# Swapping the order of two preparations before each group's first added pair, and reloading a spilled tile two pairs later

## The chip, the cores and the metric

The kernel runs on one core of a Trainium2 chip. The metric is the device time of one execution in microseconds (us). Three executions of the kernel before took 1149.12, 1149.59 and 1150.76 us; their median, 1149.59 us, is the time before. A separate execution, the one that was profiled, took 1150.18 us; its trace spans 1148.2 us from the first to the last instruction, at a granted TensorE clock of 0.997.

## The reference

One layer of an encoder on 256 tokens of width 2048, all in float32:

```
h   = rmsnorm(x, norm1_gain);  proj = h @ w_in
x   = x + concat(attention(proj), hgrn2(proj)) @ w_out
h2  = rmsnorm(x, norm2_gain)
ff  = silu(h2 @ w_gate) * (h2 @ w_up)        # 2048 -> 5632, twice
x   = x + ff @ w_down                        # 5632 -> 2048
out = rmsnorm(x, final_gain)
```

The change touches only the last three products, `w_gate`, `w_up` and `w_down`, which fill the trace from about 449 us on.

## The kernel before

**Products in parts.** Every float32 operand is held as a rounded part and a rest: `wh` and `wl` for weights, and likewise for activations. A product is three matmuls: rounded with rounded, rounded with rest, rest with rounded. Forming `wh` is a copy on ACT (ScalarE, L88); forming `wl` is a subtraction on DVE (VectorE, L89) that reads the `wh` just formed. Both handle 128x1024 elements at a time, half of a pair. Four tiles of each kind rotate.

**Pairs and groups.** The weights come in pairs: 1 MB, two 128-row slices of two 512-column blocks. The two blocks of activations (tokens 0-127, 128-255) and the two column blocks give four PSUM sums c00, c01, c10, c11. A group is a pass over all pairs of two column blocks: eleven groups `gated` for gate and up (eight pairs each), then two groups `down` (22 pairs each). A pair has one of three kinds:

- "d", ordinary: load `raw`, form `wh` and `wl` for both halves, 24 matmuls.
- "s", a pair of seven products (in the manner of Strassen) with sums and differences `ta`, `tb` of the weights formed on DVE (L747 to L749), 21 matmuls into the c and m banks.
- "a", added: as "d", but DVE forms nothing. `begin` loads the pair into `rawa`, ACT writes its negated rounded copy into `low` (L716), and a DMA issued on POOL (GpSimd) adds the weights from HBM onto it (L717), which leaves the rest. `prepare_begun` later forms `wh` from `rawa` (L727). Its matmuls with `wh` come first (16), those with `low` last (8).

Groups 1 to 10 of `gated` run `full`, that is a4, s0, d5, s1, a6, s2, s3, d7 (kind, then pair number); group 0 has ordinary pairs only. At the end of a group come the last pair's 24 matmuls, block by block, and the read-out of the banks: `spread` (L841 on ACT, L842 to L845 on DVE) reads the m banks, `block` (L852, L858, L860) the c banks.

**What sets the order.** `run_groups` prepares one pair ahead: while the matmuls of item i are written, item i+1 is prepared by `prepare`. For an "a" item, `begin` is called one item earlier still, in the `prepare` of the item before it. Each engine executes its own instructions in one order that a scheduler derives from this program text; the two L716 copies are held to their place in the text. All large loads are issued by SP in one chain (`dma`), each when its buffer is free: `raw` has three buffers, `rawa` one. A load that waits for its buffer holds up those behind it. The DMAs into `low` are issued by POOL; `low` has three buffers.

**The spilled tile.** The sum after `w_out`, `x2` (2 MB), is written to HBM early in group 0 of `gated`, because its space is needed for `hs`, and read back by two 1 MB loads `x<-x2d` at the start of `down`. It is first used at L909, after the seven "s" pairs of the first `down` group.

Of the kernel before, what the change touches and what calls it, by code (L numbers as in the profile page):

```python
# [8 lines left out]
F32 = mybir.dt.float32  # L9
# [7 lines left out]
P = 128  # L17
S = 256
NT = S // P
D = 2048  # L20
# [25 lines left out]
def hybrid_block(ctx: ExitStack, tc: tile.TileContext, x, xT, w_in, w_out, w_gu, w_down,  # L46
# [8 lines left out]
    res = ctx.enter_context(tc.tile_pool(name="res", bufs=1))  # L55
# [25 lines left out]
    def dma(o, i):  # L81
        with ExitStack() as st:
            if prev:
                st.enter_context(tc.issue_after(prev[-1]))
            prev.append(nc.sync.dma_start(o, i).ins)
# [118 lines left out]
    for t in range(NT):  # L204
        a = abp.tile([P, 4, P], F32, name=f"aT{t}")
# [234 lines left out]
    for g in range(2):  # L440
        vxs.append(abp.tile([P, 2, W], F32R, tag="t4", name="vx", bufs=NT4))
        v1s.append(abp.tile([P, W], F32, tag="ht", name="v1", bufs=3))
        pool, tag = (pacc, "acc") if g == 0 else (paux, "aux")
# [150 lines left out]
    x2 = res.tile([P, NT, D], F32, tag="res", name="x2")  # L594
# [68 lines left out]
    def row_sums(dst, hi, lo):  # L663
        n = hi.shape[1] // 2
        a = dn.tile([P, 2, 2, S], F32, tag="ta", name="a")[:, 0:n]
        sm = dn.tile([P, 4, 2, P], F32, tag="tb", name="sm")[:, :, 0:n]
        nc.vector.tensor_tensor(a, hi.rearrange("p (j k) t -> p j k t", k=2).bitcast(F32),
                                lo.rearrange("p (j k) t -> p j k t", k=2).bitcast(F32), ALU.add)
        a11, a12, a21, a22 = a[:, :, 0, 0:P], a[:, :, 1, 0:P], a[:, :, 0, P:S], a[:, :, 1, P:S]
        nc.vector.tensor_tensor(sm[:, 0], a21, a22, ALU.add)  # L670
        nc.vector.tensor_tensor(sm[:, 1], sm[:, 0], a11, ALU.subtract)
        nc.vector.tensor_tensor(sm[:, 2], a11, a21, ALU.subtract)
        nc.vector.tensor_tensor(sm[:, 3], a12, sm[:, 1], ALU.subtract)
        split(dst[:, 0], dst[:, 1], sm)
# [98 lines left out]
    def run_groups(groups, following=None):  # L773
        todo = [(gr, n) for gr in groups for n in range(len(gr.items))]

        def prepare(i):
            if i + 1 < len(todo):
                gr, n = todo[i + 1]
                if gr.items[n][0] == "a":
                    gr.begin(gr.items[n][1])  # L780
            gr, n = todo[i]
            return gr.prepare(*gr.items[n])

        steps, held = groups[0].ready or prepare(0), []
        for i, (gr, n) in enumerate(todo):
            ahead = None
            if n + 1 == len(gr.items):
                if i + 1 < len(todo):
                    ahead = prepare(i + 1)
                elif following is not None:  # L790
                    following.ready = following.prepare(*following.items[0])
                gr.run_blocks(held + steps, gr.block)
                held = []
                gr.end()
            elif n + gr.hold >= len(gr.items):
                held = held + steps
            else:
                gr.run(steps)
                seen = sum(1 for kind, _ in gr.items[:n + 1] if kind == "s")
                if gr.items[n][0] == "s" and seen == gr.ns:  # L800
                    gr.spread()
            if i + 1 < len(todo):
                steps = ahead or prepare(i + 1)
            gr.between(n)
# [6 lines left out]
    x2d = spill.tile([NT, P, D], F32, name="x2d")  # L811
    own = {"low": gu}
# [13 lines left out]
    def ff_split(ff, j):  # L826
        for i in range(2):
            pt = pair_transpose(lambda t: ff[:, t, :], i * 256)
            hi, lo, k = f_home(4 * j + 2 * i)
            ks = slice(k, k + 2)  # L830
            split(hi[:, ks, :], lo[:, ks, :], pt.rearrange("p j t n -> p j (t n)"))

    class Gated(Group):
# [31 lines left out]
        def between(self, n):  # L865
            if n == 0:
                if self.g == 0:
                    second_end()
                    for t in range(NT):
                        dma(x2d[t], x2[:, t, :])  # L870
                    own["hs"] = res.tile([P, 2, 4, FASTU, P], F32R, tag="res", name="hs")
                else:
                    ff_split(gated[self.g - 1].ff, self.g - 1)
            if self.g == 0 and 1 <= n <= (FASTU + 1) // 2:
                j0, j1 = 2 * n - 2, min(2 * n, FASTU)
                row_sums(own["hs"][:, :, :, j0:j1, :], h2[:, 2 * j0:2 * j1, 0, :], h2[:, 2 * j0:2 * j1, 1, :])
# [13 lines left out]
    def load_fg():  # L890
        fg = own["fg"]
        dma(fg, fgain.to_broadcast([P, D]))
        nc.scalar.activation(warm, fg[:, 0:1], AF.Square)
        nc.scalar.activation(warm, warm, AF.Sqrt)

    class Down(Group):
# [44 lines left out]
        def between(self, n):  # L941
            if self.g == 0:
                if n == 0:
                    x2 = own["x2"] = res.tile([P, NT, D], F32, tag="res", name="x2")
                    for t in range(NT):
                        dma(x2[:, t, :], x2d[t])
                    gup.__exit__(None, None, None)
                    late = ctx.enter_context(tc.tile_pool(name="late", bufs=1))
                    own.update(f_last=late.tile([P, 2, 4, S], F32R, name="f_last"), fg=late.tile([P, D], F32, name="fg"))
                    ff_split(gated[-1].ff, len(gated) - 1)  # L950
                elif n <= FAST // 2:
                    ks = slice(4 * (n - 1), 4 * n)
                    row_sums(sf[:, n - 1], fh[:, ks, :], fl[:, ks, :])
                elif n == FAST // 2 + 1:
                    load_fg()

    def finish(ps, t):
        x2 = own["x2"]
# [94 lines left out]
```

## Time and profile before

| What | Value |
|---|---|
| Median of three runs (lowest, highest) | 1149.59 us (1149.12, 1150.76) |
| Profiled execution, its span | 1150.18 us, 1148.2 us |
| PE busy | 1131.7 us, 99% of the span, 5381 matmuls |
| DVE busy | 916.4 us, 80% |
| ACT busy | 699.6 us, 61% |
| Moved by DMA | 248.95 MB, 217 GB/s over the span |
| One `gated` group, 1 to 10 | 42.55 us; PE busy 42.22 us, DVE 38.5 us, DMA engines 80% of the time |

PE is TensorE's matmuls; PEld is its loading of weights. A matmul of 512 columns is listed with some 390 ns, but successive ones start 227 ns apart, because they overlap; so a stall is read from the distance of two starts, not from the busy share. "Idle before, releaser" in square brackets names what an engine waited for.

### The profile page before, as it was taken

To read this page: it belongs to the slowest core of one execution; us is meant where nothing else is said; L and a number is where in the kernel's file an instruction comes from. 1 tells how busy PE (TensorE), PEld (TensorE's weight loads), DVE (VectorE), ACT (ScalarE), POOL (GpSimd) and SP (SyncE) were. 2 spreads that over 40 slices of the span, in tenths; PEclk is the share of its full clock that TensorE was granted. 3 is DMA by queue.
4 is the path that set the end of the run, shared out by engine and by line. 5 is a ranking of instruction groups with operands and counts; after the bars stand their busy time and mean duration, and the time that the engine had idled before them with its cause. 6 is when DMAs were issued, how large, how long until landed. Compare 5 with 4: busy or idle time off the path is not lost.

```text
span 1148.2 us, 14288 instructions
## 1 busy us (share of the span) xinstructions
PE 1131.7 (99%) x5381; PEld 941.1 (82%) x5381; DVE 916.4 (80%) x1166; ACT 699.6 (61%) x900; POOL 53.7 (5%) x73
## 2 busy tenths in 40 slices
PE   9999999999999999999999999999999999999996
PEld 7888888888888888887888878878878877888885
DVE  7577768947746666589889889889989998898885
ACT  7565656847645555576676676676676565555553
POOL 3300000000000000000010010010010000000000
PEclk9999999999999999999999999999999999999998
DMA  9655445554744547878778778778788756555552
GB/s 316 248 199 181 176 147 184 183 184 147 287 153 160 191 163 277 271 219 218 261 255 225 259 254 236 259 245 244 256 241 241 265 206 220 211 191 211 199 214 74
DMA packets 41397, 248.95 MB, mean 217 GB/s; under 512 B 4848, under 2 KB 5360, under 8 KB 15344
## 3 DMA queue, kind: packets, MB, share of 16 engines
q1 hardware_dynamic: 35568, 227.06, 54.1%
q0 software_dynamic: 5760, 20.97, 10.5%
q8 instruction: 42, 0.69, 0.2%
q14 instruction: 27, 0.22, 0.1%
HBM read 243.82 MB, written 4.19 MB: 216 GB/s over the span
## 4 chain that ended last, share of the span: by engine, by line
PE 93%; DVE 3%; ACT 1%; DMA 1%; issue 1%; SPq 0%; ACTq 0%; DVEq 0%
PE c L704 43%; PE m L704 13%; PE acc L169 10%; PE acc L171 5%; PE acc L146 5%; PE acc L144 5%; PE acc L145 5%; DVE wl L89 2%; PE vps L145 1%; PE ptr L315 1%; PE vps L146 1%; PE vps L144 1%; DMA x2d<-x 1%; ACT wh L88 1%; DMA raw<-in_w_in_dram 0%
## 5 line engine op out<-in xcount | busy, mean ns | idle before, releaser
L89 DVE TENSOR_TENSOR wl<-raw,wh 128x1024 fp32r<-128x1024 f32 (+1 forms) x378 | 418.8, 1122 | 134.5 <-ACT wh L88 133.2
L88 ACT ACTIVATE wh<-raw 128x1024 fp32r<-128x1024 f32 (+1 forms) x378 | 362.4, 972 | 229.5 <-PE c L704 79.2
L704 PE MATMUL c<-wh,h 128*128 128x512 f32 x928 | 275.7, 390 | 0.0
L704 PEld LDWEIGHTS c<-wh,h 128*128 128x128 f32 x928 | 173.4, 188 | 37.5 <-ACT wh L88 1.7
L169 PE MATMUL acc<-hx,wh 128*128 128x512 f32 x512 | 179.7, 395 | 0.0
L171 PE MATMUL acc<-hx,wl 128*128 128x256 f32 x512 | 142.6, 278 | 0.0
L704 PE MATMUL c<-wl,h 128*128 128x512 f32 x304 | 119.6, 394 | 3.1 <-DVE wl L89 3.1
L169 PEld LDWEIGHTS acc<-hx,wh 128*128 128x128 f32 x512 | 96.0, 188 | 21.7
L88 ACT ACTIVATE wh<-ta 128x1024 fp32r<-128x1024 f32 x55 | 58.4, 1061 | 71.4 <-PE c L704 36.3
L88 ACT ACTIVATE wh<-tb 128x1024 fp32r<-128x1024 f32 x55 | 58.3, 1061 | 63.0 <-PE c L704 34.8
L171 PEld LDWEIGHTS acc<-hx,wl 128*128 128x128 f32 x512 | 96.4, 188 | 0.1
L704 PE MATMUL c<-wh,fh 128*128 128x512 f32 x230 | 89.6, 390 | 0.4 <-ACT wh L88 0.2
L704 PE MATMUL c<-wl,fh 128*128 128x512 f32 x230 | 89.5, 389 | 0.0
L704 PE MATMUL c<-wh,fl 128*128 128x512 f32 x230 | 89.5, 389 | 0.0
L704 PE MATMUL m<-wh,hs 128*128 128x512 f32 x240 | 82.0, 389 | 0.0
L89 DVE TENSOR_TENSOR wl<-ta,wh 128x1024 fp32r<-128x1024 f32 x55 | 67.2, 1223 | 18.1 <-ACT wh L88 18.0
L704 PEld LDWEIGHTS c<-wl,h 128*128 128x128 f32 x304 | 57.0, 188 | 19.5 <-DVE wl L89 7.5
L89 DVE TENSOR_TENSOR wl<-tb,wh 128x1024 fp32r<-128x1024 f32 x55 | 67.2, 1221 | 6.7 <-ACT wh L88 4.5
L747 DVE TENSOR_TENSOR ta<-raw 128x1024 f32<-128x1024 f32 x55 | 67.2, 1221 | 6.4 <-DMA raw<-in_w_down_dram 5.8
L717 POOL DMA_DIRECT2D low<-in_w_gu_dram x40 | 34.6, 873 | 731.1 <-ACT low L716 571.2
L704 PEld LDWEIGHTS m<-wh,hs 128*128 128x128 f32 x240 | 45.1, 188 | 9.6
L704 PEld LDWEIGHTS c<-wh,fh 128*128 128x128 f32 x230 | 43.1, 188 | 10.0 <-ACT wh L88 0.6
(289 smaller groups left out, 1845.6 us busy)
## 6 DMA issues: line engine op xcount, KB each, us to landing
raw<-in_w_gu_dram SPq DMA_DIRECT2D x68, 1024.0 KB, 7.2
raw<-in_w_in_dram SPq DMA_DIRECT2D x48, 1024.0 KB, 4.8
raw<-in_w_down_dram SPq DMA_DIRECT2D x44, 1024.0 KB, 4.8
rawa<-in_w_gu_dram SPq DMA_DIRECT2D x20, 1024.0 KB, 6.4
low<-in_w_gu_dram POOLq DMA_DIRECT2D x40, 512.0 KB, 7.5
raw<-in_w_out_dram SPq DMA_DIRECT2D x16, 1024.0 KB, 4.8
raw<-in_w_in_dram SPq DMA_DIRECT2D x12, 512.0 KB, 6.0
raw<-in_w_in_dram SPq DMA_DIRECT2D x8, 256.0 KB, 5.0
```

The source lines that it names most:

```text
L88: nc.scalar.activation(hi, src, AF.Copy)
L89: nc.vector.tensor_tensor(lo, src, hi.bitcast(F32), ALU.subtract)
L144: nc.tensor.matmul(ps[t], lhsT=xh[:, tok], rhs=wh, start=kt == 0, stop=False)
L145: nc.tensor.matmul(ps[t], lhsT=xh[:, tok], rhs=wl, start=False, stop=False)
L146: nc.tensor.matmul(ps[t], lhsT=xl[:, tok], rhs=wh, start=False, stop=kt == kts - 1)
L169: nc.tensor.matmul(ps[m].rearrange("p j t -> p (j t)"), lhsT=wh[:, col], rhs=both, start=kt == 0, stop=False)
L171: nc.tensor.matmul(ps[m][:, 0, :], lhsT=wl[:, col], rhs=rhs[:, kt, 0, :], start=False, stop=kt == KD - 1)
L315: nc.tensor.transpose(pt[:, j, t, :], nat(t)[:, n0 + j * P:n0 + (j + 1) * P], ident)
L704: nc.tensor.matmul(self.bank[n], lhsT=a, rhs=b, start=self.left[n] == self.total[n], stop=self.left[n] == 1)
L717: nc.gpsimd.dma_start(out=wl.rearrange("p b n -> p (b n)"), in_=self.src[self.base + j, :, 2 * k * W:2 * (k + 1) * W], accum_op=ALU.add)
L747: nc.vector.tensor_tensor(ta, raw[:, 1:3], raw[:, 0:2], ALU.subtract)
```

## The change

In `prepare`, an ordinary pair is now prepared (its load, its two `wh`, its two `wl`) before the `begin` of a following added pair; before, `begin` came first. For the other kinds the order is as it was, so a6, which follows s1, is begun as before. The place where "d" is followed by "a" is the end of a group: d7 of groups 0 to 9, followed by a4 of the next group. The reload of `x2` moves from after pair 0 to after pair 2 of the first `down` group.

```diff
         def prepare(i):
-            if i + 1 < len(todo):
-                gr, n = todo[i + 1]
-                if gr.items[n][0] == "a":
-                    gr.begin(gr.items[n][1])
             gr, n = todo[i]
-            return gr.prepare(*gr.items[n])
+            nxt, m = todo[i + 1] if i + 1 < len(todo) else (None, 0)
+            steps = gr.prepare(*gr.items[n]) if gr.items[n][0] == "d" else None
+            if nxt and nxt.items[m][0] == "a":
+                nxt.begin(nxt.items[m][1])
+            return steps or gr.prepare(*gr.items[n])
...
                 if n == 0:
-                    x2 = own["x2"] = res.tile([P, NT, D], F32, tag="res", name="x2")
-                    for t in range(NT):
-                        dma(x2[:, t, :], x2d[t])
                     gup.__exit__(None, None, None)
...
                 elif n == FAST // 2 + 1:
                     load_fg()
+                if n == 2:
+                    x2 = own["x2"] = res.tile([P, NT, D], F32, tag="res", name="x2")
+                    for t in range(NT):
+                        dma(x2[:, t, :], x2d[t])
```

The first place is ACT at the end of a group, from the last `tb` of s3 to the first `wh` of s0 in the next group. `wh<-raw ... x2` are the two halves of d7, `low<-rawa` and `wh<-rawa` belong to a4. Before:

```order
L88 ACTIVATE wh<-tb 128x1024
L841 COPY ff<-m_4956 128x512
L716 ACTIVATE low<-rawa 128x1024 x2
L88 ACTIVATE wh<-raw 128x1024 x2
L727 ACTIVATE wh<-rawa 128x1024 x2
L88 ACTIVATE wh<-raw 128x512
```

and after:

```order
L88 ACTIVATE wh<-tb 128x1024
L841 COPY ff<-m_4956 128x512
L88 ACTIVATE wh<-raw 128x1024 x2
L716 ACTIVATE low<-rawa 128x1024 x2
L727 ACTIVATE wh<-rawa 128x1024 x2
L858 ACTIVATE ff<-ff,rst_3175 128x512
```

The two negated copies go two places back, and the two `wh` of d7 two places forward.

The second place is DVE at the same point: `uv` and `ff` at L842 to L845 read the m banks of the group that ends, L852 its c banks. Before:

```order
L89 TENSOR_TENSOR wl<-tb,wh 128x1024
L842 TENSOR_TENSOR uv<-m_4958,ff 128x512
L89 TENSOR_TENSOR wl<-raw,wh 128x1024
L843 TENSOR_TENSOR uv<-m_4957,uv 128x512
L844 TENSOR_TENSOR ff<-m_4959,uv 128x512
L89 TENSOR_TENSOR wl<-raw,wh 128x1024
L845 TENSOR_TENSOR uv<-m_4957,ff 128x512
L852 TENSOR_TENSOR ff<-c_4891,ff 128x512
L852 TENSOR_TENSOR uv<-c_4892,uv 128x512
L852 TENSOR_TENSOR ff<-c_4893,ff 128x512
L860 SCALAR_TENSOR_TENSOR ff<-uv,rst_3175,ff 128x512
L852 TENSOR_TENSOR uv<-c_4894,uv 128x512
```

and after:

```order
L89 TENSOR_TENSOR wl<-tb,wh 128x1024
L89 TENSOR_TENSOR wl<-raw,wh 128x1024 x2
L842 TENSOR_TENSOR uv<-m_4958,ff 128x512
L843 TENSOR_TENSOR uv<-m_4957,uv 128x512
L844 TENSOR_TENSOR ff<-m_4959,uv 128x512
L852 TENSOR_TENSOR ff<-c_4891,ff 128x512
L845 TENSOR_TENSOR uv<-m_4957,ff 128x512
L852 TENSOR_TENSOR uv<-c_4892,uv 128x512
L852 TENSOR_TENSOR ff<-c_4893,ff 128x512
L860 SCALAR_TENSOR_TENSOR ff<-uv,rst_3175,ff 128x512
L89 TENSOR_TENSOR wl<-raw,wh 128x512
L852 TENSOR_TENSOR uv<-c_4894,uv 128x512
```

Both `wl` of d7 now stand ahead of L842; before, they stood behind it and between the others. The first `wl` of the next pair (128x512, s0) now stands ahead of the read of c_4894, which is c11.

The third place is SP's queue from the last groups of `gated` into `down`; `x` is the tile `x2`. Before:

```order
L85 DMA raw<-in_w_gu_dram 128x2048 x3
L85 DMA rawa<-in_w_gu_dram 128x2048
L85 DMA raw<-in_w_gu_dram 128x2048 x4
L85 DMA raw<-in_w_down_dram 128x2048 x2
L85 DMA x_7752<-x2d 128x2048 x2
L85 DMA raw<-in_w_down_dram 128x2048 x5
L85 DMA fg<-in_fgain_dram 128x2048
```

and after:

```order
L85 DMA raw<-in_w_gu_dram 128x2048 x2
L85 DMA rawa<-in_w_gu_dram 128x2048
L85 DMA raw<-in_w_gu_dram 128x2048 x4
L85 DMA raw<-in_w_down_dram 128x2048 x4
L85 DMA x_7858<-x2d 128x2048 x2
L85 DMA raw<-in_w_down_dram 128x2048 x3
L85 DMA fg<-in_fgain_dram 128x2048
```

Ahead of `rawa` for a4 there is now one load more, that of d7 (x4 instead of x3 between two `rawa`, and x2 instead of x3 after it); the reload has moved behind two more loads of `down`. PE's order changes with DVE's: d7's matmuls now run block by block, where before the scheduler had put four matmuls with `wh` ahead of the first with `wl`.

## The prediction

> **What bounds the kernel now.** I read the page first, for the engine that carries the span.
>
> ```profile
> span 1148.2 us, 14288 instructions
> PE 1131.7 (99%) x5381; PEld 941.1 (82%) x5381; DVE 916.4 (80%) x1166; ACT 699.6 (61%) x900; POOL 53.7 (5%) x73
> ...
> PE 93%; DVE 3%; ACT 1%; DMA 1%; issue 1%; SPq 0%; ACTq 0%; DVEq 0%
> ```
>
> PE carries 93% of the chain. A change elsewhere is worth only the PE stalls that it removes or makes, so I looked next for these, in the list of waits and, by place, in the chain in order of time.
>
> ```profile
> PEld c L704 <- DVE wl L89: 7.8, 11, 0.8
> ...
> DVE uv L842 <- PE m L704: 15.9, 9, 1.8
> ```
>
> ```profile
> 517.71 1.23 DVE wl L89
> ...
> 687.86 1.23 DVE wl L89
> ...
> 858.01 1.23 DVE wl L89
> ```
>
> The chain leaves PE for a `wl` once per group, nine times from 517.71 to 858.01, every 42.55 us: at the ends of groups 1 to 9. L842 waits for PE nine times as well. The timeline of one such place, with weight loads left out, shows why:
>
> ```profile
> 684.26 1.23 DVE L89 TENSOR_TENSOR wl<-tb,wh 128x1024 fp32r<-128x1024 f32 x1
> 684.60 2.01 ACT L716 ACTIVATE low<-rawa 128x1024 fp32r<-128x1024 f32 x2
> 686.06 1.80 POOL L717 DMA_DIRECT2D low<-in_w_gu_dram  x2 [21.35 <-ACT low L716]
> 686.50 2.00 ACT L88 ACTIVATE wh<-raw 128x1024 fp32r<-128x1024 f32 x2
> 687.25 0.69 DVE L842 TENSOR_TENSOR uv<-m,ff 128x512 f32<-128x512 f32 x1 [1.77 <-PE m L704]
> 687.45 1.35 PE L704 MATMUL c<-wh,h 128*128 128x512 f32 x5
> 687.86 1.22 DVE L89 TENSOR_TENSOR wl<-raw,wh 128x1024 fp32r<-128x1024 f32 x1
> 688.40 2.00 ACT L727 ACTIVATE wh<-rawa 128x1024 fp32r<-128x1024 f32 x2
> 689.13 0.51 PE L704 MATMUL c<-wl,h 128*128 128x512 f32 x1 [0.33 <-DVE wl L89]
> 689.47 0.63 PE L704 MATMUL c<-wh,h 128*128 128x512 f32 x2
> ...
> 697.42 1.98 PE L704 MATMUL c<-low,h 128*128 128x512 f32 x8
> ```
>
> ACT makes a4's two negated copies (684.60) before d7's `wh` (686.50). DVE, done with `tb` at 685.49, has nothing it may do: its next instruction, L842, needs the last m bank and starts at 687.25. d7's first `wl` follows at 687.86 and ends at 689.08, and PE, which has used up its four `wh` matmuls, starts at 689.13.
>
> The size of the stall: matmuls start (1.98 - 0.39) / 7 = 0.227 us apart in the last row. Of the five from 687.45 the last starts at 687.45 + (1.35 - 0.39) = 688.41, so the next was due at 688.64 and came at 689.13: 0.49 late. The one after it came 0.34 later instead of 0.227: 0.11 more. Together **0.61 us per group, 5.5 us in nine groups**. This is the most that the first edit can give.
>
> **The change part by part.**
>
> *d7 ahead of a4's copies.* Nothing is added or removed. ACT's two pairs of copies change places: both take 1.9 us from start to start (684.60 to 686.50 to 688.40), so d7's `wh` move to 684.60 and 685.55, L716 to 686.50 and 687.45, and L727 stays at 688.40. DVE can form d7's `wl` at 685.7 to 688.1, in the time in which it now waits for the m bank. PE wants the first at about 687.9 and the second at 688.6. So the stall goes: -5.5 us. Group 10, which no added pair follows, already runs in the new order and shows it:
>
> ```profile
> 898.38 2.36 DVE L89 TENSOR_TENSOR wl<-raw,wh 128x1024 fp32r<-128x1024 f32 x2 [0.21 <-ACT wh L88]
> ...
> 900.13 0.62 PE L704 MATMUL c<-wh,h 128*128 128x512 f32 x2
> ...
> 900.59 0.39 PE L704 MATMUL c<-wl,h 128*128 128x512 f32 x1
> 900.65 0.69 DVE L842 TENSOR_TENSOR uv<-m,ff 128x512 f32<-128x512 f32 x1
> ```
>
> Two `wl` stand before L842, and PE passes from 900.13 to 900.59 at its 0.23 us per matmul.
>
> *SP's order.* d7's load no longer stands behind `rawa`, which waits for L727 of a6 to free its buffer.
>
> ```profile
> 668.27 0.68 DVE L749 TENSOR_TENSOR tb<-raw,tb 128x512 f32<-128x512 f32 x1
> ...
> 672.05 0.33 SPq L85 DMA_DIRECT2D rawa<-in_w_gu_dram  x1
> 672.47 10.60 SPq L85 DMA_DIRECT2D raw<-in_w_gu_dram  x3
> ```
>
> Its own buffer, last read by s1, is free at 668.95; so it goes 3.5 us earlier, and `rawa` still goes at 672.05. ACT wants `rawa` at 686.50 now. This costs nothing by itself. In group 10, where no `rawa` stands in the way, a6's copies meet such an early load already, and no wait of PE for a copy stands in the list of waits.
>
> *The copies `low` come later.* This is the price. Both are issued by POOL after L716, so 1.90 us later, while PE comes to them 0.61 us sooner. PE wants the second at its fifth `low` matmul, 697.42 + 4 x 0.227 = 698.33. When it is issued, and what such copies take from issue to landing (least, median, most), stands in the tile's own view; here it is for this place (the second issue precisely 0.94 us after 686.06, at 687.00), for the ends of two earlier groups, and for a6's second copy alone:
>
> ```profile
> L717 POOL DMA_DIRECT2D low<-in_w_gu_dram x2: 847/854/860, 686.1 to 687.0; - x2
> ...
> DMA to landing us min/median/max: 5.3/7.1/8.8
> ```
>
> ```profile
> DMA to landing us min/median/max: 5.6/6.5/7.3
> ```
>
> ```profile
> DMA to landing us min/median/max: 5.8/7.4/9.0
> ```
>
> ```profile
> L717 POOL DMA_DIRECT2D low<-in_w_gu_dram x1: 870/870/870, 663.8 to 663.8; - x1
> ...
> DMA to landing us min/median/max: 10.5/10.5/10.5
> ```
>
> The second copy has 698.33 - 687.00 = 11.33 us now and 11.33 - 1.90 - 0.61 = **8.82 us after**. The first copy lands after 5.3 to 5.8 us and has more in hand. The second takes 7.3 to 9.0 us at a group's end, and 10.5 us in a6, where SP issues a load beside it:
>
> ```profile
> 663.77 0.33 SPq L85 DMA_DIRECT2D raw<-in_w_gu_dram  x1
> ...
> 690.42 0.33 SPq L85 DMA_DIRECT2D rawa<-in_w_gu_dram  x1
> ```
>
> At a group's end the next load is issued 690.42 - 687.00 = 3.4 us after the second copy, in a6 at the same time. After the change L727 still frees `rawa` at 690.4, so the distance is 690.4 - 688.9 = 1.5 us. Bounds: 7.3 us if the loads do not touch the copy; 9.4 us on a straight line between (0, 10.5) and (3.4, 8.05, the mean of 7.3 and 8.8). If each us of earlier load costs the copy one us, it is 10.5 - 1.5 = 9.0 us. I take 9.0, because it is also near this place's own 8.8. PE then waits 9.0 - 8.82 = 0.18 us in each of nine groups, **+1.6 us**; bounds 0 and 9 x (9.4 - 8.82) = +5.2 us. The Trainium skill ("DMA: Bandwidth & Descriptors", "Anatomy of one DMA") gives a fit for copies of this path, 2.0 us and the bytes at 436 GB/s: 3.2 us for 0.5 MB, and PE would wait for neither, a sum of -5.5 us. The trace does not agree; its shortest copy here took 5.3 us, and the measured ones decide.
>
> *The banks' read-out.* L842 starts at about 688.0 instead of 687.25, but the chain of DVE then has no `wl` in it. The narrowest point is c11, which the next group's PE needs.
>
> ```profile
> 691.96 0.63 ACT L88 ACTIVATE wh<-raw 128x512 fp32r<-128x512 f32 x1 [1.56 <-PE c L704]
> ```
>
> s0's first `wh` waits for d7's last use of a buffer, the 21st instead of the 15th matmul of d7, so it comes at some 692.6; its `wl` at 693.3 stands ahead of c11's read, which ends near 694.6. PE writes that bank 31 matmuls after d7's start at 687.67, at 694.7. A margin of 0.1 us: 0, at worst a few tenths, and not on top of the wait for `low`, which comes 2.9 us later on the same PE.
>
> *The reload.* Two loads move behind those of down's pairs 2 and 3.
>
> ```profile
> 899.87 0.80 SPq L85 DMA_DIRECT2D x<-x2d  x2
> ```
>
> ```profile
> DVE wl L89 <- ACT wh L88: 0.4, 2, 0.2
> ```
>
> ```profile
> 909.88 1.07 ACT L88 ACTIVATE wh<-raw 128x1024 fp32r<-128x1024 f32 x1 [1.33 <-PE c L704]
> ...
> 918.26 1.06 ACT L88 ACTIVATE wh<-raw 128x1024 fp32r<-128x1024 f32 x1 [1.66 <-PE c L704]
> ```
>
> From 898 to 950 us DVE waits 0.4 us in all (second fence), and for no load; pair 2 and pair 4 are taken up when PE frees a buffer (909.88, 918.26). So earlier loads give nothing. Pair 4's load now has two reloads ahead of it, at most 2 x 2.6 us more (1.05 MB at 406 GB/s, the rate of a busy stretch), and must be there by 918.26. I take 0; bounds -0.4 us (DVE's idle time) and +0.9 us (pair 4 late, DVE being full).
>
> Sum: -5.5 + 1.6 + 0 + 0 = -3.9 us, from the profiled execution's 1150.18 us to 1146.3. The median of the runs stands 0.6 us lower, so there **1145.7 us**.
>
> The rate of 406 GB/s is from the view of windows; the last two columns are the share of the DMA engines and GB/s:
>
> ```profile
> 694.00:698.00 4.00, 4.00 (x19) 3.31 (x18) 4.00 (x7) 1.67 (x2) 0.00 (x0) 1.00 0.98 406
> ```
>
> The DMA engines are full (0.98) just where the copy is to land.
>
> **The rivals.** *The copy takes the stall's place, and more.* If the second copy takes 10.5 us as in a6, PE waits 1.68 us per group and the kernel loses 9 x (1.68 - 0.61) = 9.6 us: 1159.2. It is slower at all from 9.43 us on, and measurably from 9.7. For it: the full DMA engines. Against it: at this distance much of the copy is through before the loads begin. The Trainium skill (the same page, "Queues, rings and completion order") has each DMA engine take turns, packet by packet, between the queues that have work, which is the sharing that this rival needs; 10.5 against 7.3 us agrees with it. *The gain is eaten.* Between 9.1 and 9.7 us the wait is 0.3 to 0.9 us per group, and what is left lies between +2.3 and -2.3 us: about 1149. *The edit does not remove the wait*, because d7's `wl` waits for something else, or the read-out of c11 takes up the time: 1149.6. Against it stands group 10.
>
> **How the numbers follow.** Two medians of this kernel can be told apart from about 0.2%, 2.3 us. The forecast, a gain of 2.3 to 5.5 us, has 0.63; the gain eaten 0.20; no effect 0.09; the slower rival 0.08. The range runs from the full gain, 1149.59 - 5.5 = 1144.1, with 0.3 for a gain in `down`, to the upper bound of the copy, -5.5 + 5.2 = -0.3 or 1149.3, with half of pair 4's bound: 1143.8 to 1149.7. The likeliest case alone spans 1144.1 to 1147.3. Faster 0.63, the same 0.29, slower 0.08.
>
> **What would show it.** Right: no `wl` in the chain at the nine places, a group's length near 42.1 us, L842 behind two `wl` without 1.8 us of idle time, L716 some 1.9 us later against PE. Wrong: a wait of PE's weight load for a DMA at the fifth `low` matmul, a group of 42.5 us or more, or a wait for c11's read. For the reload: the same stalls of PE in `down`, and `wh` of pair 4 still released by PE.

## The result, and the profile after

The changed kernel is slower by 0.8%: 1158.82 us (median of four runs, 1157.92 to 1162.06) against 1149.97 us for the kernel before in the same measurement (four runs, 1149.12 to 1150.76). The ratio is 1.0082, 95% interval 1.0061 to 1.0104. The profiled execution took 1157.92 us, with a span of 1156.1 us against 1148.2 us: 7.9 us more.

The list of waits of PE's weight load (total, times, longest) names another releaser than before:

```profile
PEld c L704 <- DMA low<-in_w_gu_dram: 15.0, 9, 2.6
PEld c L704 <- DVE uv L852: 2.3, 9, 0.3
...
PEld c L704 <- DVE wl L89: 1.0, 2, 0.6
```

The wait for `wl`, 7.8 us in eleven places before, is down to 1.0 us in two. In its stead PE waits nine times for a DMA into `low`. The timeline of the same group end as in the prediction, other rows left out:

```profile
687.72 2.01 ACT L88 ACTIVATE wh<-raw 128x1024 fp32r<-128x1024 f32 x2
...
688.82 2.36 DVE L89 TENSOR_TENSOR wl<-raw,wh 128x1024 fp32r<-128x1024 f32 x2 [0.21 <-ACT wh L88]
...
689.63 2.00 ACT L716 ACTIVATE low<-rawa 128x1024 fp32r<-128x1024 f32 x2
...
691.09 1.80 POOL L717 DMA_DIRECT2D low<-in_w_gu_dram  x2 [23.67 <-PE c L704]
691.10 0.68 DVE L842 TENSOR_TENSOR uv<-m,ff 128x512 f32<-128x512 f32 x1
...
693.55 0.33 SPq L85 DMA_DIRECT2D rawa<-in_w_gu_dram  x1
...
693.97 8.77 SPq L85 DMA_DIRECT2D raw<-in_w_gu_dram  x2
...
700.02 1.07 PE L704 MATMUL c<-low,h 128*128 128x512 f32 x4
...
703.23 0.98 PE L704 MATMUL c<-low,h 128*128 128x512 f32 x3 [2.14 <-DMA low<-in_w_gu_dram]
```

The edit did what it says: both `wl` run at once, L842 behind them no longer idles, and the matmuls of d7 follow each other without a break. But the fifth `low` matmul, due at 700.02 + 4 x 0.227 = 700.93, starts at 703.23, 2.30 us late. It waits for the second copy, issued at 692.03, here in the tile's own view (least, median, most are the same for one copy):

```profile
L717 POOL DMA_DIRECT2D low<-in_w_gu_dram x1: 857/857/857, 692.0 to 692.0; - x1
...
DMA to landing us min/median/max: 11.2/11.2/11.2
```

This is the worst of the nine; the others take 10.0 to 10.3 us and stop PE for 1.1 to 1.4 us. The first and the last of the nine stops:

```profile
529.20 1.19 PE L704 MATMUL c<-low,h 128*128 128x512 f32 x4 [0.97 <-DMA low<-in_w_gu_dram]
```

```profile
876.42 0.97 PE L704 MATMUL c<-low,h 128*128 128x512 f32 x3 [1.18 <-DMA low<-in_w_gu_dram]
```

The eight groups between them take (876.42 - 529.20) / 8 = 43.40 us each against 42.54 us before. From start to start the nine stops are 12.6 us in all. Behind each of them the next matmuls start up to 0.34 us apart instead of 0.227, as behind the old wait, which adds 0.12 us a group, 1.1 us in all. Less the 5.5 us of the old wait that makes +8.2 us against 7.9 us in the span, so these stops are the whole loss, to 0.3 us.

### The profile page after: what moved, and what is told of

Read it like the earlier page. It is cut to its first block, busy times and chain, and to the rows that moved or that the text cites. A ratio compares the mean times of both kernels' runs of the same rounds, so it can differ in the third digit from the quotient of the medians.

```text
span 1156.1 us, 14299 instructions
## 1 busy us (share of the span) xinstructions
PE 1131.3 (98%) x5381; PEld 942.1 (81%) x5381; DVE 924.0 (80%) x1166; ACT 703.8 (61%) x900; POOL 53.5 (5%) x73
## 3 DMA queue, kind: packets, MB, share of 16 engines
q0 software_dynamic: 5760, 20.97, 10.3%
## 4 chain that ended last, share of the span: by engine, by line
PE 60%; issue 28%; DVE 4%; DMA 2%; POOL 2%; ACT 2%; SPq 0%; POOLq 0%; ACTq 0%; DVEq 0%
PE c L704 19%; PE acc L169 10%; PE acc L171 5%; PE acc L146 5%; PE acc L144 5%; PE acc L145 5%; PE m L704 5%; POOL low L717 2%; DVE wl L89 2%; PE vps L145 1%; PE vps L146 1%; PE vps L144 1%; DMA low<-in_w_gu_dram 1%; ACT wh L88 1%; DMA x2d<-x 1%
## 5 line engine op out<-in xcount | busy, mean ns | idle before, releaser
L704 PE MATMUL c<-low,h 128*128 128x512 f32 x160 | 42.2, 396 | 11.2 <-DMA low<-in_w_gu_dram 11.2
```

What stands on the lines that cost most here:

```text
L704: nc.tensor.matmul(self.bank[n], lhsT=a, rhs=b, start=self.left[n] == self.total[n], stop=self.left[n] == 1)
```

## The experiments

The theory: the whole loss is the second copy, and it is late because it meets the next loads on the DMA engines. Rivals: the reload costs the time; a copy issued this late is slow whatever stands beside it; something else in the new order (the read-out of c11) costs it. All kernels compute the whole reference. "Budget" below is the time from the issue of the second copy to the moment at which PE is due at the fifth `low` matmul, and "distance" the time from that issue to the issue of the next load; both, and the ranges of the copy's time, are from the nine group ends of each trace. Ratios are to the kernel before, measured in the same set.

### Each edit alone

The first kernel is the changed one with the reload back at its old place:

```diff
                 if n == 0:
+                    x2 = own["x2"] = res.tile([P, NT, D], F32, tag="res", name="x2")
+                    for t in range(NT):
+                        dma(x2[:, t, :], x2d[t])
...
-                if n == 2:
-                    x2 = ...
```

> The first edit alone: d7's parts ahead of the next pair's copies, the reload of the residual at its old place. Theory (the copy): the whole loss comes from the second accumulating copy into low, which is issued 1.9 us later, meets the next loads after 1.5 us instead of 3.4 us and so takes 10.0 to 11.2 us against a budget of 8.8 us. Then this kernel takes as long as the changed one, 1158 to 1160 us, with PE waits of 1.1 to 2.3 us at the fifth low matmul of nine groups. Rival (the reload): the loss, or much of it, lies in the down projection, where two loads are put behind those of later pairs; then this kernel takes 1146 to 1153 us.

The second is the kernel before with the same lines moved the other way.

> The second edit alone: the order of before, with the reload two pairs further on. Theory (the copy): 1149 to 1151 us, no difference from before; PE waits about 2 us in all in the first pairs of down, as in both kernels. Rival (the reload): 1154 us or more, with PE waits in down for wh or for a load.

Measured: the order alone 1158.27 us, ratio 1.0072 (1.0059 to 1.0084); the reload alone 1150.93 us, ratio 1.0002 (0.9993 to 1.0011). The order alone shows the same wait in its list as the changed kernel:

```profile
PEld c L704 <- DMA low<-in_w_gu_dram: 15.0, 9, 2.1
```

PE's waits in the stretch from 898 to 965 us, before and then with the reload alone:

```profile
PE m L704 <- DVE wl L89: 1.0, 1, 1.0
PE m L704 <- ACT wh L88: 0.4, 1, 0.4
```

```profile
PE m L704 <- ACT wh L88: 0.7, 1, 0.7
PE m L704 <- DVE wl L89: 0.6, 1, 0.6
```

1.4 us and 1.3 us: the reload is free, and the loss is all in the order.

### The loads later, the copy where it is

This is the changed kernel with a 64-byte transfer on SP's queue ahead of the next loads, which must wait for the activations of the group just ended:

```diff
         def begin(self, j):
+            if j == 6:
+                dma(late_d[self.g], gated[self.g - 1].ff[0:1, 0, 0:16])
             raw, low = own["low"].tile([P, 4, W], F32, name="rawa"), []
...
+    late_d = spill.tile([FF // W, 1, 16], F32, name="late_d")
     own = {"low": gu}
```

> The changed kernel with one thing more: a transfer of 64 bytes, from the activations of the group that has just ended to a scratch place in DRAM, stands on SP's queue ahead of the next loads. It waits for those activations, so the loads are issued 3 us or more after the second copy instead of 1.5 us; the copy itself is issued as late as in the changed kernel. Theory (the copy meets the loads): the second copy lands after 7.3 to 9.0 us, as before the change; PE waits at most 0.2 us per group for it, and the time is 1144 to 1149 us. Rival (a copy issued at this place, 1.9 us later, is slow whatever loads stand beside it): 10 us and more, waits of 1.1 to 2.3 us, 1157 to 1160 us.

Measured: 1145.86 us, ratio 0.9960 (0.9947 to 0.9972). Loads and `low` matmuls in its timeline, and its second copy of the same group, issued at 686.66 (line numbers are two higher):

```profile
691.09 0.24 SPq L85 DMA_DIRECT2D late_d<-ff  x1
...
691.42 0.33 SPq L85 DMA_DIRECT2D rawa<-in_w_gu_dram  x1
...
694.61 1.98 PE L704 MATMUL c<-low,h 128*128 128x512 f32 x8
```

```profile
L719 POOL DMA_DIRECT2D low<-in_w_gu_dram x1: 857/857/857, 686.7 to 686.7; - x1
...
DMA to landing us min/median/max: 7.3/7.3/7.3
```

The loads come 4.8 us behind the copy, the copy takes 7.3 us (7.0 to 8.7 over the nine), and the eight matmuls run through. Its budget is 8.9 us, the same as the changed kernel would have without a wait. So the copy's place is not what slows it. Adding a transfer that delays two loads turned the loss into a gain.

The view of the DMA queues shows the meeting. Packets, MB and the share of the 16 engines' time; q0 carries the copies, q1 the loads, q8 instructions. First the changed kernel from 697.03 to 701.03, 5 to 9 us after the copy's issue:

```profile
q1 hardware_dynamic: 102, 0.84, 52.5%
q0 software_dynamic: 101, 0.40, 50.3%
q8 instruction: 1, 0.02, 1.4%
```

The two queues get as many packets, 101 and 102, as they would by turns of one packet. From 6.5 to 10 us after the issue, in the kernel before, the changed kernel, and the one with later loads:

```profile
q1 hardware_dynamic: 172, 1.29, 93.7%
q0 software_dynamic: 11, 0.02, 2.6%
```

```profile
q1 hardware_dynamic: 134, 0.97, 67.7%
q0 software_dynamic: 72, 0.23, 33.7%
```

```profile
q1 hardware_dynamic: 196, 1.46, 99.3%
q0 software_dynamic: 10, 0.01, 1.5%
```

In the first and the third the copy is all but through by then and the loads have the engines nearly to themselves. In the changed kernel 0.23 MB of it are still under way, beside the loads.

### One of the two loads later

The same small transfer stands between the two loads, so that only s1's load is put off:

```diff
             dma(raw.rearrange("p b n -> p (b n)"), self.src[self.base + j])
+            if j == 6:
+                dma(late_d[self.g], gated[self.g - 1].ff[0:1, 0, 0:16])
```

> As the run with the loads later, but the small transfer stands between the two loads: rawa's load is issued 1.5 us after the second copy, as in the changed kernel, and only the load of s1's weights comes later. Theory A (one load beside the copy is enough, since the load's 8 packets on each DMA engine outlast the 6 that the copy still has there): the copy takes 9.7 us or more, PE waits 0.9 us or more per group, 1154 to 1159 us. Theory B (it takes both loads, a queue share of two in three): the copy takes 8.7 to 9.4 us, PE waits up to 0.6 us, 1145 to 1151 us.

Measured: 1161.26 us, ratio 1.0101 (1.0085 to 1.0116), a little over the upper end of theory A.

```profile
PEld c L704 <- DMA low<-in_w_gu_dram: 15.5, 9, 2.7
```

The copies take 9.9 to 11.3 us, as with both loads beside them. One load is enough, and theory B falls.

### The next pair begun between the halves of d7

```diff
...
                 for k in range(2):
                     parts = halves_of(raw[:, 2 * k:2 * k + 2])
+                    if k == 0 and mid:
+                        mid()
...
+            begin = (lambda: nxt.begin(nxt.items[m][1])) if nxt and nxt.items[m][0] == "a" else None
+            if gr.items[n][0] == "d":
+                return gr.prepare(*gr.items[n], mid=begin)
...
```

> The next pair is begun between the two halves of d7 (ACT: wh, two negated copies, wh), so the copies go out about 0.95 us later than before instead of 1.9 us. Theory (the copy meets the loads): distance to the next load some 2.5 us, budget some 9.8 us, the second copy takes some 9 us (between 8.0 at 3.4 us and 10.3 at 1.5 us), and PE waits at most 0.3 us for it; d7's second wl comes as late as before, so up to 0.6 us per group of the old wait stays: 1146 to 1152 us. Rival (a copy issued late is slow whatever is beside it): the second copy takes 10 us or more here too, PE waits for it 0.3 us or more per group beside the old wait, 1153 us or more.

Measured: 1147.45 us, ratio 0.9973 (0.9963 to 0.9984).

```profile
686.02 1.05 ACT L88 ACTIVATE wh<-raw 128x1024 fp32r<-128x1024 f32 x1
...
688.99 0.33 SPq L85 DMA_DIRECT2D rawa<-in_w_gu_dram  x1
...
695.40 2.28 PE L704 MATMUL c<-low,h 128*128 128x512 f32 x8
```

The second copy goes out at 686.52, so the distance is 2.47 us, and it takes 9.9 us (9.1 to 9.9 over the nine) against a budget of 9.8: it just fits, and PE waits once, 0.2 us, in this very group. The part of the expectation that kept up to 0.6 us of the old wait was wrong. With this program text the scheduler also puts PE's matmuls on d7's second half behind those on the first half of the next blocks, so the second `wl` is wanted later. PE's order at the end of a group, where c_4891 to c_4894 are c00 to c11; the `wl` of c_4891 for the second half stands behind the first matmul of c_4894, where the changed kernel has it ahead of c_4892:

```order
L704 MATMUL c_4893<-wl,h_3174 128x512
L704 MATMUL c_4893<-wh,h_3174 128x512 x2
L704 MATMUL c_4894<-wh,h_3174 128x512
L704 MATMUL c_4891<-wl,h_3174 128x512
L704 MATMUL c_4891<-wh,h_3174 128x512
L704 MATMUL c_4892<-wl,h_3174 128x512
```

### PE takes the copies later

```diff
...
             else:
-                gr.run(steps)
+                if gr.items[n][0] == "a":
+                    gr.run(steps[:8])
+                    rest = steps[8:]
+                else:
+                    gr.run(steps + rest)
+                    rest = []
```

> The changed order, but PE runs the eight matmuls on low of each added pair after the matmuls of the next item (21 matmuls, some 5 us more in hand). Theory (the copy): the copies still take 10 us and more, nothing waits for them, and the nine waits for wl are gone as well: 1150.0 less 9 x 0.61, and up to 9 x 0.25 back for the read-out of c11, so 1144 to 1147 us. Rival (the loss is not PE's wait for low but something else that the new order costs, the read-out of the banks or the reload): 1150 us or more.

Measured: 1146.38 us, ratio 0.9967 (0.9955 to 0.9979). Here the copies still take 10.0 to 11.1 us at a distance of 1.5 us, but the budget is 13.2 us and no wait for a DMA into `low` is left in the middle groups. The nine waits for `wl` shrink and do not vanish, as was expected: the weight loads wait 0.3 us at each place, and PE's starts there are 0.16 us late instead of 0.61. The eight `low` matmuls come in three pieces between those of s0; the first and the last piece in the same group, both without a wait:

```profile
698.69 0.86 PE L704 MATMUL c<-low,h 128*128 128x512 f32 x3
...
702.34 0.62 PE L704 MATMUL c<-low,h 128*128 128x512 f32 x2
```

So a copy of 10 us costs nothing by itself; it costs what it lacks of its budget.

### The copies early

a4 is begun two items ahead, behind s3's load and ahead of s3's parts:

```diff
...
+            if kind == "s" and i + 2 < len(todo) and todo[i + 2][1] == 0 and todo[i + 2][0].items[0][0] == "a":
+                far = todo[i + 2][0]
+                return gr.prepare(*gr.items[n], mid=lambda: far.begin(far.items[0][1]))
...
```

> The next added pair is begun two items ahead, in the preparation of s3, so the negated copies and the accumulating copies go out some 8 us before d7's parts are formed, and d7's parts stand first at the group's end. Theory (the copy): nothing waits for low, nor for wl at the nine places; 1150.0 less 9 x 0.61, with up to 9 x 0.25 back for the read-out of c11: 1144 to 1147 us. Rival (ACT pays for it: two negated copies of 0.95 us ahead of s3's parts make PE wait there): 1148 us or more, with a new wait for s3's wh or wl.

Measured: 1145.39 us, ratio 0.9958 (0.9946 to 0.9971). Its list holds no wait for `low`. Of the two below, both of weight loads and at most 0.3 us each, the second is for c11, which the changed order brings; the first, put down to a part of the activations (`fl`), lies in s0 and stands in the list with the later loads as well:

```profile
PEld m L704 <- DVE fl L89: 2.4, 9, 0.3
PEld c L704 <- DVE uv L860: 2.3, 9, 0.3
```

The copies take 10.1 to 13.0 us with loads beside them, and have 17.3 us or more. ACT's two copies ahead of s3's parts make no wait of PE. This version is faster than both kernels, and so, by their intervals, are the ones with later loads, with the copies between the halves and with `low` taken later. This one and the one with later loads are too near to each other to be ranked.

### Two of them together

> Two of the earlier kernels together: the next pair begun between the halves of d7, and PE's matmuls on low after those of the next item. Theory (in each of the two PE waits for nothing in the middle groups, which last 41.9 us): no further gain, 1144 to 1147.5 us. Rival (the two gains add): 1142 us or less.

Begun between the halves, and `low` taken later: 1150.65 us, ratio 1.0003 (0.9994 to 1.0012). Neither expectation holds; the gain is gone. In its list of waits and its timeline:

```profile
PEld c L704 <- ACT wh L88: 6.4, 11, 0.9
PEld m L704 <- ACT wh L88: 5.3, 10, 1.1
```

```profile
683.34 1.06 ACT L88 ACTIVATE wh<-tb 128x1024 fp32r<-128x1024 f32 x1 [2.64 <-DVE tb L751]
...
687.62 1.04 ACT L88 ACTIVATE wh<-raw 128x1024 fp32r<-128x1024 f32 x1
...
688.72 0.77 PEld L704 LDWEIGHTS c<-wh,h 128*128 128x128 f32 x4 [0.53 <-ACT wh L88]
```

DVE is late with s3's `tb`, and ACT idles 2.64 us for it. It idles as long in the kernel with `low` taken later alone, but there both `wh` of d7 come ahead of the negated copies, and PE loses only 0.16 us. Here the second comes behind them: it ends at 688.66, 0.5 us after PE's weight load wants it, and PE loses 0.38 us there. The second row is of s0, where PE loses another 0.31 us. Groups last 42.48 us, as before the change. Why DVE comes late to `tb` was not traced further.

## Why the prediction was wrong

*The stall of 0.61 us goes.* Right. In three kernels in which nothing else takes its place the gain is 0.33% to 0.42% of 1150 us, 3.8 to 4.8 us, against 5.5 us; the intervals reach from 2.4 to 6.2 us.

*The budget, 8.82 us, and the distance, 1.5 us.* Right: 8.9 us where PE does not wait for the copy (the later loads), and 1.52 us.

*The copy's time, 9.0 us with bounds of 7.3 and 9.4.* This is the step that failed. The copies took 10.0 to 11.2 us, mean 10.2. With this mean the sum is 9 x (10.2 - 8.9) - 5.5 = +6.2 us, which is the sign and most of the size. The 1.1 us behind the stops bring it to +7.3 us: the stall of 0.61 us was reckoned with what comes behind it, the wait for the copy without. What the runs show of the copy by the distance to the next load:

| Kernel | Distance (us) | Second copy to landing (us) |
|---|---|---|
| loads later | 4.8 | 7.0 to 8.7 |
| before | 3.4 to 3.5 | 7.3 to 9.0, once 11.3 |
| between the halves | 2.5 | 9.1 to 9.9 |
| between the halves, `low` later | 2.5 | 9.4 to 11.4 |
| changed | 1.5 to 1.6 | 10.0 to 11.2 |
| changed, one load later | 1.5 to 1.6 | 9.9 to 11.3 |
| a6 before, groups 2 to 9 | -0.1 | 10.0 to 10.5 |

It is no straight line. The means are 7.6 us at 4.8 us of distance, 8.0 at 3.4 (without the 11.3), 9.5 and 10.3 at 2.5, 10.2 at 1.5 and 10.2 at -0.1: nearly the whole rise lies between 3.4 and 1.5 us, and the same distance of 2.5 us gives two means. The line between (0, 10.5) and (3.4, 8.05) spread it over the whole stretch, and "one us for one us", counted down from 0, did the same more steeply. The line also left out the 9.0 us that stands among the three group ends shown; with it the mean at 3.4 us is 8.4 and the upper bound 9.6 instead of 9.4, past the 9.43 from which the kernel is slower, and still under what was measured.

The packets give the reason for most of it. In the trace of the changed kernel the loads' first packets start 4.1 to 4.6 us after the copy's issue, and 97 to 117 packets of the copies are then still to come, 0.40 to 0.48 MB; in the kernel before and in the one with later loads they start at 6.0 to 6.6 us, and 0 to 22 are. A load's first packet comes 2.5 to 3.2 us behind its issue in the changed kernel and the one before, but 1.3 to 1.6 us with the loads later, so the distance of the issues tells only roughly when the packets meet. The first row of q0 above has 101 packets. On 16 engines that is 6.3 packets each, at 0.503 x 4 us x 16 / 101 = 0.32 us some 2.0 us alone and twice that in turns: by this estimate 2 us more than the 8 us of before. That turns are taken is what the Trainium skill says ("DMA: Bandwidth & Descriptors", "Queues, rings and completion order"), and the 101 and 102 packets agree; I had cited it for the rival and not worked it out in packets. Its fit for one DMA of this path (the same page, "Anatomy of one DMA") gave an estimate of 3.2 us; no copy here took less than 5.2 us.

The rise between 3.4 and 2.5 us is steeper than this mean over the engines explains; there the last few packets decide. When `low` is taken later as well, 32 to 62 packets are left as the loads begin, no more than between the halves alone (29 to 69), and yet the copies take longer. Their tail is long, as in the slow copy of before that is told of below; here are the queues from 524.40 to 528.00 in that trace:

```profile
q1 hardware_dynamic: 195, 1.47, 98.7%
q0 software_dynamic: 6, 0.02, 3.1%
```

The loads have the engines, and the copy's last packets come one at a time, at 0.63 us from start to start (once 0.79), which is two turns of 0.32 us. So they seem to stand on one engine that has fallen behind; the views do not name the engine, and what puts it behind is open. One thing goes with it: in the four kernels with a distance of 1.5 us, seven of the eight copies above 10.3 us have a packet of the instruction queue beside them, as the slowest one of the changed kernel has (q8 above: 1.4% of 16 engines in 4 us, 0.9 us of one engine). Other copies with such a packet took 9.9 to 10.3 us, and whether it is the cause was not tested.

There was a warning in the trace of before. At the end of group 1 the second copy took 11.3 us at a distance of 3.5 us and PE waited for it:

```profile
528.12 0.77 PEld L704 LDWEIGHTS c<-low,h 128*128 128x128 f32 x4 [0.20 <-DMA low<-in_w_gu_dram]
```

I gave 7.3 to 9.0 us for group ends, and so missed one copy in nine that lay above the bound of 9.4. This row also stands against the prediction's word that no wait of PE for a copy is in the list of waits: there is one, of 0.2 us. 12 packets of that copy were left when the loads began.

*The rival.* "The copy takes the stall's place, and more" with 10.5 us and 1159.2 us is what happened. That its loss, 9.6 us, comes so near the measured 8.9 us is partly luck: the copies took 0.3 us less than in a6, 2.3 us in nine groups, and the 1.1 us behind the stops were not in it. I held against it that much of the copy is through before the loads begin. That is so of both copies together, but of the second, 0.5 MB, some 0.40 MB were still to come.

*The read-out of c11.* It does bring nine waits of 0.3 us, all of weight loads. In the kernel with later loads, which has them too, a group lasts 41.98 us against 42.54 - 0.61 = 41.93: about nothing, as said.

*The gain eaten.* The figures of this rival are a little off: a gain of 2.3 us goes with a copy of 9.2 us, and 9.1 us would leave 3.0. Nothing hangs on it.

*The reload.* Right, from the run with it alone: 0.0002 with bounds of -0.0007 and +0.0011, -0.8 to +1.3 us.

## What to carry to other kernels

When a transfer is issued later, ask first what will be on the DMA engines by then, and count its packets that are still to come: each of them costs two turns while another queue has work (0.63 us here), and a few on a late engine are enough to hold up the landing. A step on an idle engine can be the one that the time hangs on, because it frees the buffer that lets the next load go. Where the collision is known, delaying the loads that nobody needs yet can be as good as hurrying the copy, if the first of them is delayed too.

## What the runs showed of the hardware

A packet of the accumulating copy holds half as much as one of a load and takes as long: 0.40 MB in 101 packets at 50.3% of four us on 16 engines, 0.32 us each, and 0.84 MB in 102 packets at 52.5%, 0.33 us each. Beside such copies the engines are full and move less: 345 GB/s in the changed kernel from 698.53 to 702.03, and 419 GB/s in the same stretch after the copy's issue with the loads later, in the view of windows (last two columns: share of the DMA engines, GB/s):

```profile
698.53:702.03 3.50, 2.56 (x12) 1.74 (x10) 3.43 (x5) 1.01 (x1) 0.00 (x0) 1.00 1.01 345
```

```profile
693.16:696.66 3.50, 3.50 (x19) 2.86 (x18) 3.43 (x5) 1.02 (x1) 0.00 (x0) 1.00 1.01 419
```
